# One-core decoder layer: order of the score matmuls, weight halves in slots of their own, convolution taps dealt out anew, the last norm's small matmuls later

## The chip, the cores and the metric

The kernel runs on one core of one Trainium2 chip. The metric is the device time of one execution in microseconds (us), lower is better. Engines are called as in the profile: PE multiplies matrices, DVE, ACT and POOL work on vectors, SP issues most of the DMAs.

## The reference, cut to what matters

One layer over 256 tokens of width 1024, all in float32: a mixer, cross attention and a gated feed-forward part (FFN), each behind an RMS norm.

```
h = rms_norm(x);  x = x + hybrid_mixer(h) ; x = x + cross_attention(rms_norm(x), mem); x = x + swiglu(rms_norm(x))
# hybrid_mixer
(u_conv, q, kc, vc, ks, vs, kw, vw, g_nsa_heads, g_conv, g_attn) = split(h @ w_in)
conv_out = conv_module(u_conv)     # a*sigmoid(g), depthwise causal convolution of 31 taps, layer norm, silu, @ pw_w
nsa_out  = nsa_attention(q, ...)   # 16 heads of 64; compressed, selected and window branch, gated
y = sigmoid(g_conv) * conv_out + sigmoid(g_attn) * nsa_out;   return y @ w_out
# swiglu
a, b = split(h @ w_in);  return (silu(a) * b) @ w_out
```

## The kernel before, in words

**Weights.** A projection is cut into chunks of 256 output columns, named after what they make: k0 to k3, u0 to u7, kc, vc, q0 to q3, ks, kw, vs, vw, ga0 to ga3, gc0 to gc3, pw0 to pw3, wo, xq, v, xo, f0 to f21. Each chunk arrives in two halves (`_0`, `_1`, 512 KB each). `split` (L195) makes two fp32r tiles of a half: ACT copies the high part (`f_0h`, L205), and DVE or POOL subtracts it to leave the low part (`f_0l`, L208). `rows` and `sweep` (L285 to L305, matmuls on L297) then multiply: 8 matmuls of 128x128 by 128x256 for high times high, 8 for high times low input, 8 for low weights times high input; 48 for a chunk. Those of one half are in one row of the views as x8.

**Slots.** Most weight halves rotate through five buffers, `whi` and `wlo`. `set_apart` (L220) gives one half two slots of its own instead, in which the high part begins 64 floats and the low part 112 floats behind the slot's start. Before, these are k3_0, xq1_0, xq2_0, xo0_1, ks_0 and f2_0.

**Order.** `in_line` and `behind` tie matmuls to the one written before them; the rest is placed by a scheduler with priorities, and each engine takes its own instructions in order.

**Scores.** `scores(hp)` (L840) makes the scores of two heads against the keys (kdh, kdl are their high and low parts): `later_half` the second 128 queries of a head (tiles `s`, 512 columns, L852), the loop on L858 the first 128 of both (256 columns each, L860). DVE adds the bias and takes minima (L865, L871), ACT takes the exponential (L886), DVE normalises (L889 to L896), PE transposes the weights (`pt_a`, `pt_b`, L907) and multiplies them with the values (`o`). `scores(0)` stands in front of ga3, later ones stand between pieces of gc and v (v is the value projection of the cross attention).

**Convolution taps.** 8 blocks of 128 channels, 31 taps each, between 30 and 160 us. `taps_v` (L488) is DVE's chain of multiply-adds (L494) with every third product of the later taps from ACT (L486) and an addition on DVE (L508). `taps_g` (L513) is POOL's: products by ACT, additions on L530, for the first ON_G taps of channel blocks 6 and 7. LEAD and the tuple in the call of `convolve` (L570) say how many steps are dealt out behind which u chunk.

**Small fp32 matmuls** interrupt the stream of fp32r ones: the relative bias tables (`rel_ps` L579, `cb_ps` L587), branch gates and compressed scores (`gt_ps` L805, `cs_ps` L793), the norm in front of the FFN (`rn` sums over partitions, L379; `sp` spreads the root, L397) and the 16 transposes of the residual (`fo`, L1236).

Of the kernel before, what the change touches and what calls it, by code (L numbers as in the profile page):

```python
# [118 lines left out]
def tile_hybrid_block(  # L119
# [113 lines left out]
    set_apart("xq1_0", "LL")  # L233
    set_apart("xq2_0", "LL")
    set_apart("xo0_1", "LL")
    set_apart("ks_0", "L11", "L13")
    set_apart("f2_0", "L9", "L0")

    def behind(*marks):
# [118 lines left out]
    def newton(v, name):  # L358

        I32 = mybir.dt.int32  # L360
        g, t = (small(f"{c}_{name}", [P, 2]) for c in ("nr", "nt"))
        nc.vector.tensor_scalar(out=t.bitcast(I32), in0=v.bitcast(I32), scalar1=1, scalar2=None, op0=ALU.arith_shift_right)
        nc.vector.tensor_scalar(out=g.bitcast(I32), in0=t.bitcast(I32), scalar1=-1.0, scalar2=float(0x5F3759DF), op0=ALU.mult,
                                op1=ALU.add)
        for _ in range(4):
            nc.gpsimd.tensor_tensor(out=t, in0=g, in1=g, op=ALU.mult)
            nc.gpsimd.tensor_tensor(out=t, in0=t, in1=v, op=ALU.mult)
            nc.gpsimd.tensor_scalar(out=t, in0=t, scalar1=-0.5, scalar2=1.5, op0=ALU.mult, op1=ALU.add)
            nc.gpsimd.tensor_tensor(out=g, in0=g, in1=t, op=ALU.mult)
        return g  # L370
# [109 lines left out]

    yt = long("yt", 6)

    def product_of(j, t, to, n=2):

        for i in range(n):
            nc.scalar.activation(to[:, i], vt[j + i][:, t:t + S], AF.Identity, scale=col(PP_DW + TAPS * (j + i), t),  # L486
                                 bias=col(PP_DB, j + i) if t == 0 else 0.0)

    def taps_v(j, ts, out, lead=0):

        acc = aux(f"yp{j}", [P, 2, S], "pt", 2)

        def step(i, t, to):
            nc.vector.scalar_tensor_tensor(out=to[:, i], in0=vt[j + i][:, t:t + S], scalar=col(PP_DW + TAPS * (j + i), t),  # L494
                                           in1=acc[:, i], op0=ALU.mult, op1=ALU.add)

        early, late = ts[1:1 + lead], ts[1 + lead:]
        product_of(j, ts[0], acc, 1)
        for t in early:
            step(0, t, acc)  # L500
            yield
        product_of(j + 1, ts[0], acc[:, 1:2], 1)
        for n, t in enumerate(late):
# [37 lines left out]
    def by_turns(a, b, alone):  # L541

        yield from islice(a, alone)
        for _ in a:
# [1 line left out]
            yield next(b, None)  # L546
        yield from b

    on_v = chain(by_turns(taps_v(0, taps, yt[:, 0:2], LEAD), taps_v(2, taps, yt[:, 2:4]), 18 + LEAD),
                 by_turns(taps_v(4, taps, yt[:, 4:6]), taps_v(6, taps[ON_G:], part67), 0))  # L550
    on_g = chain(taps_g(6, taps[:ON_G]), joined(6, part67))

# [12 lines left out]
    for j in range(NB):  # L565
        ps = gemm(f"u{j}", h)
        sg = small(f"sg{j}", [P, S], tag="sg", bufs=3)
        act = nc.scalar.activation(sg, ps[:, 1], AF.Sigmoid)
        vec = nc.vector.tensor_tensor(out=vt[j][:, PAD:], in0=ps[:, 0], in1=sg, op=ALU.mult)
        convolve((LEAD, 8, 10, 10, 10, 10, 10, 10)[j], 0, act, vec)  # L570


    tables = long("tables", 12, (P, RT_END + len(CGROUPS) * P))
# [1 line left out]
    with behind(loads["u6_1"]):  # L575
        nc.sync.dma_start(relt, rel)
        nc.sync.dma_start(cbt, cb)
    rel_ps = aux("rel_ps", [P, 384], "s", 2)
    nc.tensor.matmul(rel_ps, lhsT=relt[:, 0:P], rhs=relt[:, P:512],  # L579
                     start=True, stop=True)  # L580

# [173 lines left out]
            js = slice(j, j + 2)  # L755
            nc.vector.tensor_tensor(out=yt[:, js], in0=yt[:, js], in1=rl.unsqueeze(1).to_broadcast([P, 2, S]), op=ALU.mult)

    def gate(j):

        ps = bank(f"ps_ga{j}")  # L760
        for i in range(2):
            sweep(ps, halved(f"ga{j}", i), h, i)
        return nc.scalar.activation(sga[:, 2 * j:2 * j + 2], ps, AF.Copy if j == 3 else AF.Sigmoid)

    sums = small("sums", [P, HEADS, 2, 2])
# [21 lines left out]
    def compressed_scores(ct):  # L787
# [7 lines left out]
        last[:] = [mm]  # L795
        nc.vector.tensor_tensor(out=nsc, in0=cs_ps, in1=nsc, op=ALU.add)

    four[0] = ""
    ct = compressed_products()
    gate(0)  # L800
    compressed_scores(ct)
    gt_ps = aux("gt_ps", [P, 2, ng], "o", 1)

    for tb in range(2):
        nc.tensor.matmul(gt_ps[:, tb], lhsT=sgn[:, tb * P:tb * P + P], rhs=cpt[:, CP_GS:CP_GS + ng], start=tb == 0, stop=tb == 1)  # L805
    sgt = small("sgt", [P, 2, ng], tag="sg", bufs=3)
    nc.scalar.activation(sgt, gt_ps, AF.Sigmoid)
    nc.vector.reciprocal(igc, sgt[:, :, 0:HEADS])
    vec = nc.vector.reciprocal(igd.rearrange("p h t b -> p t b h"),
                               sgt[:, :, HEADS:3 * HEADS].rearrange("p t (b h) -> p t b h", b=2))  # L810
    vcm = small("vcm", [P, GROUPS, 2, HD], F32R, tag="wg")
    for k in range(2):
        nc.scalar.activation(vcm[:, :, k], f(vcs), AF.Copy, scale=cpt[:, CP_HM + k:CP_HM + k + 1])
    gate(1)
    mark = gate(2)
    stacked = long("stacked", 9, (P, 2, NB, 4, 32), F32R)

# [22 lines left out]
    def scores(hp):  # L840

        g = hp // 2
        nbp = bias_of(hp)
        s0 = aux(f"s0_{hp}", [P, 2, 2, P], "s0", 1)
        p0 = small(f"p0_{hp}", [P, 2, 2, P], tag="p0", bufs=2)
        s1s, p1 = [], []

        def later_half(hd):
            s1 = aux(f"s1_{hd}", [P, 2, S], "s", 2)
            with in_line():  # L850
                for i, t in enumerate((kdh, kdl)):
                    mm = nc.tensor.matmul(s1, lhsT=qh(hd, 1), rhs=t[:, g].rearrange("p b t -> p (b t)"), start=i == 0, stop=i == 1)  # L852
            last[:] = [mm]
            s1s.append(s1)

        later_half(2 * hp)
        for k, hd in enumerate(heads_of(hp)):
            with in_line():  # L858
                for i, t in enumerate((kdh, kdl)):
                    mm = nc.tensor.matmul(s0[:, k], lhsT=qh(hd, 0), rhs=t[:, g, :, 0:P], start=i == 0, stop=i == 1)  # L860
        last[:] = [mm]
        later_half(2 * hp + 1)
        for k, hd in enumerate(heads_of(hp)):
# [12 lines left out]
        return p0, p1  # L876
# [677 lines left out]
```

## Time and profile before

| | |
|---|---|
| median of 3 runs | 531.22 us (530.62 to 531.57) |
| the profiled execution | 528.97 us, of which the span from first to last instruction 527.2 us |
| PE busy in the span | 520.1 us (99%) |
| DVE, ACT, POOL busy | 442.3, 368.4, 147.4 us |
| granted PE clock, mean | 0.997 |

The profiled execution is 2.25 us below the median; differences are worked out in its time and then put on the median. A busy PE means that an instruction is in it, not that it runs at its best rate, so the distance from start to start of the same instructions has to be read beside the busy share.

### The profile page before, as it was taken

The numbers are of one execution on the slowest core, as the hardware profiler recorded it, in microseconds if no ns is written. First come the engines' busy times: TensorE is split into PE (matmuls) and PEld (weight loads), VectorE is DVE, ScalarE is ACT, GpSimd is POOL, SyncE is SP. The second block draws the span as 40 slices with busy tenths as digits, with TensorE's granted clock in tenths as the row PEclk, the third lists the DMA queues.
The fourth block names the chain that finished last, engine by engine and source line by source line (L and its number), as shares of the span: only waits on it lengthen the run. The fifth ranks groups of instructions, "written<-read, shape, count | busy, mean of one in ns | idle before, by whom it ended". The sixth has DMA issues, their size and how long they took to land.

```text
span 527.2 us, 11194 instructions
## 1 busy us (share of the span) xinstructions
PE 520.1 (99%) x4319; PEld 502.4 (95%) x4319; DVE 442.3 (84%) x861; ACT 368.4 (70%) x671; POOL 147.4 (28%) x105
## 2 busy tenths in 40 slices
PE   9999999999999999999999999999999999999995
PEld 8999999999899999999999999999999999988884
DVE  4887899999999999984969685688988786689996
ACT  5678784999967899789648675565665555557743
POOL 0019889999995000330004000310000000000002
PEclk9999999999999999999999999999999999999998
DMA  8947966544545436224667542368665665625402
GB/s 315 410 168 250 322 202 212 165 161 153 166 160 184 160 127 208 88 81 160 222 217 274 192 156 99 109 197 300 229 219 192 197 201 188 201 93 159 162 0 81
DMA packets 29445, 97.20 MB, mean 184 GB/s; under 512 B 3152, under 2 KB 5456, under 8 KB 29136
## 3 DMA queue, kind: packets, MB, share of 16 engines
q1 hardware_dynamic: 28816, 95.44, 53.9%
q10 hardware_dynamic: 576, 1.05, 0.5%
q8 instruction: 34, 0.56, 0.4%
q14 instruction: 19, 0.16, 0.1%
HBM read 95.23 MB, written 1.25 MB: 183 GB/s over the span
## 4 chain that ended last, share of the span: by engine, by line
PE 98%; DVE 1%; ACT 0%; issue 0%; ACTq 0%
PE ps_f L297 23%; PE ps_u L297 8%; PE fo L1313 6%; PE ps_v L297 4%; PE ps_gc L297 4%; PE ps_ga L297 4%; PE ps_q L297 4%; PE ps_xq L297 4%; PE ps_pw L297 4%; PE ps_wo L297 4%; PE fos L1313 4%; PE ps_k L297 3%; PE ps_xo L297 3%; PE ps_xo L1198 2%; PE o L920 1%; PE s L852 1%
## 5 line engine op out<-in xcount | busy, mean ns | idle before, releaser
L494 DVE SCALAR_TENSOR_TENSOR yp<-vt,ppt,yp 128x256 f32<-128x256 f32 x144 | 64.2, 485 | 6.3 <-ACT yp L486 4.6
L1382 POOL TENSOR_TENSOR x<-xs,gf 128x512 f32<-128x512 f32 x2 | 2.6, 1302 | 168.3 <-issue 168.3
L297 PE MATMUL ps_f<-g,f_1h 128*128 128x256 f32 x352 | 44.4, 277 | 0.0
L297 PE MATMUL ps_f<-g,f_0h 128*128 128x256 f32 x352 | 43.9, 277 | 0.0
L297 PEld LDWEIGHTS ps_f<-g,f_1h 128*128 128x128 f32 x352 | 41.9, 188 | 0.0
L297 PEld LDWEIGHTS ps_f<-g,f_0h 128*128 128x128 f32 x352 | 41.8, 188 | 0.0
L205 ACT ACTIVATE f_0h<-f 128x1024 fp32r<-128x1024 f32 x22 | 23.4, 1062 | 18.9 <-issue 15.5
L886 ACT ACTIVATE p<-p,mins 128x128 f32<-128x128 f32 (+1 forms) x64 | 28.3, 449 | 10.2 <-DVE mins L865 10.0
L208 DVE TENSOR_TENSOR f_1l<-f,f_1h 128x1024 fp32r<-128x1024 f32 x22 | 27.4, 1247 | 5.6 <-ACT f_1h L205 5.6
L208 DVE TENSOR_TENSOR f_0l<-f,f_0h 128x1024 fp32r<-128x1024 f32 x22 | 27.3, 1243 | 3.2 <-ACT oxh L346 2.2
L205 ACT ACTIVATE f_1h<-f 128x1024 fp32r<-128x1024 f32 x22 | 23.2, 1060 | 9.4 <-PE ps_f L297 7.9
L486 ACT ACTIVATE vw<-vt,ppt 128x256 f32<-128x256 f32 x60 | 26.6, 499 | 0.6 <-DVE yp L508 0.5
L1272 DVE TENSOR_TENSOR ab<-ps_f,rf 128x512 f32<-128x512 f32 x22 | 15.2, 689 | 11.6 <-PE ps_f L297 11.6
L297 PE MATMUL ps_f<-g,f_1l 128*128 128x256 f32 x176 | 23.6, 277 | 0.0
L297 PE MATMUL ps_f<-g,f_0l 128*128 128x256 f32 x176 | 23.6, 276 | 0.0
L208 POOL TENSOR_TENSOR u_0l<-u,u_0h 128x1024 fp32r<-128x1024 f32 x5 | 12.0, 2404 | 37.5 <-ACT u_0h L205 37.5
L297 PEld LDWEIGHTS ps_f<-g,f_1l 128*128 128x128 f32 x176 | 21.7, 188 | 0.0
L297 PEld LDWEIGHTS ps_f<-g,f_0l 128*128 128x128 f32 x176 | 21.6, 188 | 0.0
L530 POOL TENSOR_TENSOR yt<-yt,vw 128x512 f32<-128x512 f32 x15 | 20.5, 1367 | 0.1
L508 DVE TENSOR_TENSOR yp<-yp,vw 128x512 f32<-128x512 f32 x28 | 19.4, 695 | 0.7
L748 POOL TENSOR_TENSOR ssum<-ssum,sq 128x512 f32<-128x512 f32 x3 | 4.7, 1580 | 44.9 <-ACT sq L747 44.7
L1274 ACT ACTIVATE sl<-ab 128x256 f32<-128x256 f32 x22 | 9.1, 417 | 11.0 <-DVE ab L1272 10.9
(845 smaller groups left out, 1667.4 us busy)
## 6 DMA issues: line engine op xcount, KB each, us to landing
f<-in_wst_dram SPq DMA_DIRECT2D x44, 512.0 KB, 4.4
u<-in_wst_dram SPq DMA_DIRECT2D x14, 512.0 KB, 6.9
for<-in_wfo_dram SPq DMA_DIRECT2D x14, 512.0 KB, 3.8
q<-in_wst_dram SPq DMA_DIRECT2D x8, 512.0 KB, 4.9
ga<-in_wst_dram SPq DMA_DIRECT2D x8, 512.0 KB, 3.3
gc<-in_wst_dram SPq DMA_DIRECT2D x8, 512.0 KB, 3.8
v<-in_wst_dram SPq DMA_DIRECT2D x8, 512.0 KB, 3.1
pw<-in_wst_dram SPq DMA_DIRECT2D x8, 512.0 KB, 4.6
```

The source lines that it names most:

```text
L205: copies = [nc.scalar.activation(hi[:, at:at + n], w[:, at:at + n], AF.Copy) for at in range(0, shape[1], n)]
L208: low = eng.tensor_tensor(out=lo[:, at:at + n], in0=w[:, at:at + n], in1=f(hi[:, at:at + n]), op=ALU.subtract)
L297: mm = nc.tensor.matmul(ps[:, b], lhsT=lhsT, rhs=rhs, start=row + b + kb == 0, stop=kb == NB - 1 and row == 2 and b == 1)
L486: nc.scalar.activation(to[:, i], vt[j + i][:, t:t + S], AF.Identity, scale=col(PP_DW + TAPS * (j + i), t), bias=col(PP_DB, j + i) if t == ...
L494: nc.vector.scalar_tensor_tensor(out=to[:, i], in0=vt[j + i][:, t:t + S], scalar=col(PP_DW + TAPS * (j + i), t), in1=acc[:, i], op0=ALU.mu ...
L508: nc.vector.tensor_tensor(out=to, in0=acc, in1=pr, op=ALU.add)
L530: nc.gpsimd.tensor_tensor(out=y, in0=y, in1=pr, op=ALU.add)
L886: exp.append(nc.scalar.activation(t, t, AF.Exp, scale=-1.0, bias=mins[:, hd, qb, br:br + 1], accum_out=sums[:, hd, qb, br:br + 1]))
L1198: nc.tensor.matmul(qs[:, b], lhsT=parts[m, 1][wi][:, k, cs], rhs=x[xi][:, 4 + k], start=False, stop=k == 3 and row == 2 and b == 1)
L1272: nc.vector.tensor_tensor(out=ab, in0=ps, in1=rf.unsqueeze(1).to_broadcast([P, 2, S]), op=ALU.mult)
L1274: silu = nc.scalar.activation(sl, ab[:, 0], AF.Silu)
L1313: mm = nc.tensor.matmul(o[:, cs], lhsT=t[x], rhs=w[y][:, cs], start=start and n == 0, stop=stop and n == 2)
```

## The change

`scores` issues the four 512-column matmuls of both heads first and ends with the four of 256 columns. q3_0, ga3_0 and pw0_1 get slots of their own, ks_0 goes back to the common ones. `rel_ps` takes another PSUM bank. The branch gates and compressed scores move from between ga0 and ga1 into the middle of ga1. Three taps of channel blocks 6 and 7 go from ACT and POOL to DVE; the first taps of the leading chains are computed by DVE instead of ACT, and the second leading chain leads by 7 instead of 10. One Newton step of four is left out of a reciprocal root on POOL. The norm in front of the FFN is issued inside f0 and f1 rather than in front of them.

```
-ON_G = 16
-LEAD = 10
+ON_G = 13
+LEAD, DEALT = 10, (10, 11, 12, 12, 12, 12, 12, 12)
...
-    set_apart("ks_0", "L11", "L13")
+    set_apart("q3_0", "L11", "L13")
+    set_apart("ga3_0", "L13", "L9")
+    set_apart("pw0_1", "L10", "L14")
...
-        for _ in range(4):
+        for _ in range(3):
...
+        def first_of(j, i, to):
+            nc.vector.tensor_scalar(out=to[:, i], in0=vt[j + i][:, 0:S], scalar1=col(PP_DW + TAPS * (j + i), 0),
+                                    scalar2=col(PP_DB, j + i), op0=ALU.mult, op1=ALU.add)
...
-        product_of(j, ts[0], acc, 1)
+        if lead:
+            first_of(j, 0, acc)
+        else:
+            product_of(j, ts[0], acc)
...
-        product_of(j + 1, ts[0], acc[:, 1:2], 1)
+        if lead:
+            first_of(j, 1, acc)
...
-    on_v = chain(by_turns(taps_v(0, taps, yt[:, 0:2], LEAD), taps_v(2, taps, yt[:, 2:4]), 18 + LEAD),
+    on_v = chain(by_turns(taps_v(0, taps, yt[:, 0:2], LEAD), taps_v(2, taps, yt[:, 2:4], 7), sum(DEALT[:2])),
...
-        convolve((LEAD, 8, 10, 10, 10, 10, 10, 10)[j], 0, act, vec)
+        convolve(DEALT[j], 0, act, vec)
...
-    rel_ps = aux("rel_ps", [P, 384], "s", 2)
+    rel_ps = aux("rel_ps", [P, 384], "o", 1)
...
+    def between_gates():
+        branch_gates()
+        compressed_scores(ct)
...
     gate(0)
-    compressed_scores(ct)
...
+    gate(1, between_gates)
...
         later_half(2 * hp)
+        later_half(2 * hp + 1)
         for k, hd in enumerate(heads_of(hp)):
...
-        later_half(2 * hp + 1)
...
-    rf = small("rf", [P, S], tag="vw", bufs=4)
-    nc.scalar.activation(rf, spread(rnorm(acc2, "3"), "3"), AF.Copy)
...
+    for _ in range(7):
+        next(firsts)
+    with in_line():
+        r3 = rnorm(acc2, "3")
+    for _ in range(5):
+        next(firsts)
+    with in_line():
+        r3 = spread(r3, "3")
```

On PE, at the first scores, between ga2 and ga3 (`s_1` and `s_0` on the 512-column lines are the second halves of the two heads). Before:

```order
L297 MATMUL ps_ga_2154<-hh,ga_1l 128x256 x8
L852 MATMUL s_0_2222<-kdh,qt 128x512
L852 MATMUL s_0_2222<-kdl,qt 128x512
L860 MATMUL s_0_2220<-kdh,qt 128x256
L860 MATMUL s_0_2220<-kdl,qt 128x256
L860 MATMUL s_0_2220<-kdh,qt 128x256
L860 MATMUL s_0_2220<-kdl,qt 128x256
L852 MATMUL s_1_2229<-kdh,qt 128x512
L852 MATMUL s_1_2229<-kdl,qt 128x512
L297 MATMUL ps_ga_2242<-hh,ga_0h 128x256 x8
```

And of the change at the same place:

```order
L299 MATMUL ps_ga_2144<-hh,ga_1l 128x256 x8
L872 MATMUL s_0_2212<-kdh,qt 128x512
L872 MATMUL s_0_2212<-kdl,qt 128x512
L872 MATMUL s_1_2215<-kdh,qt 128x512
L872 MATMUL s_1_2215<-kdl,qt 128x512
L881 MATMUL s_0_2210<-kdh,qt 128x256
L881 MATMUL s_0_2210<-kdl,qt 128x256
L881 MATMUL s_0_2210<-kdh,qt 128x256
L881 MATMUL s_0_2210<-kdl,qt 128x256
L299 MATMUL ps_ga_2232<-hh,ga_0h 128x256 x8
```

The same eight matmuls stand there; the last one in front of the next projection has 256 columns instead of 512.

On PE, from the FFN's first chunk to its third (g is the FFN's input, `fo` the transposes of the residual). Before, the norm's two pieces and all 16 transposes lie ahead of f2:

```order
L297 MATMUL ps_f_4790<-g_4482,f_1h 128x256 x7
L379 MATMUL rn_4764<-ones,acc_4483 128x2 x2
L297 MATMUL ps_f_4790<-g_4482,f_1h 128x256 x6
...
L397 MATMUL sp_4770<-cpt,r_4767 128x128 x2
L297 MATMUL ps_f_4858<-g_4482,f_1h 128x256 x9
L297 MATMUL ps_f_4858<-g_4482,f_1l 128x256 x8
L1236 MATMUL fo_0_4935<-cpt,x_4481 128x128 x4
L1236 MATMUL fo_1_4936<-cpt,x_4481 128x128 x4
L1236 MATMUL fo_0_4937<-cpt,x_4481 128x128 x4
L1236 MATMUL fo_1_4938<-cpt,x_4481 128x128 x4
L297 MATMUL ps_f_4955<-g_4482,f_0h 128x256 x16
```

Of the change, the end of the same place (12 of the transposes have gone ahead into f0):

```order
L399 MATMUL sp_4893<-cpt,r_4844 128x128 x2
L299 MATMUL ps_f_4941<-g_4468,f_0h 128x256 x14
L299 MATMUL ps_f_4941<-g_4468,f_0l 128x256 x8
L299 MATMUL ps_f_4941<-g_4468,f_1h 128x256 x2
L1254 MATMUL fo_0_4923<-cpt,x_4467 128x128 x4
L299 MATMUL ps_f_4941<-g_4468,f_1h 128x256 x14
L299 MATMUL ps_f_4941<-g_4468,f_1l 128x256 x8
```

The last four transposes now lie behind f2_0, the half with slots of its own, and no such half follows in the FFN.

On DVE, the last instructions ahead of the first score reduction (L865, in the change L885; yp and yt belong to the taps). Before:

```order
L208 TENSOR_TENSOR gc_0l<-gc_0_2329,gc_0h 128x1024
L494 SCALAR_TENSOR_TENSOR yp_1277<-vt_368,ppt,yp_1277 128x256 x4
L208 TENSOR_TENSOR gc_1l<-gc_1_2359,gc_1h 128x1024
L508 TENSOR_TENSOR yt<-yp_1277,vw_30_1976 128x512
L208 TENSOR_TENSOR gc_0l<-gc_0_2434,gc_0h 128x1024
L865 ISA p_0_2221,mins<-s_0_2220,nb_2217 128x128
```

Of the change:

```order
L208 TENSOR_TENSOR gc_0l<-gc_0_2319,gc_0h 128x1024
L518 TENSOR_TENSOR yp_1194<-yp_1194,vw_27_1967 128x512
L820 RECIPROCAL igc<-sgt 128x32
L821 RECIPROCAL igd<-sgt 128x4x16
L808 TENSOR_TENSOR nsc<-cs_ps,nsc 128x512
L500 SCALAR_TENSOR_TENSOR yp_1194<-vt_368,ppt,yp_1194 128x256
L208 TENSOR_TENSOR gc_1l<-gc_1_2349,gc_1h 128x1024
L500 SCALAR_TENSOR_TENSOR yp_1194<-vt_368,ppt,yp_1194 128x256 x3
L208 TENSOR_TENSOR gc_0l<-gc_0_2424,gc_0h 128x1024
L518 TENSOR_TENSOR yt<-yp_1194,vw_30_1975 128x512
L208 TENSOR_TENSOR gc_1l<-gc_1_2454,gc_1h 128x1024
L885 ISA p_0_2211,mins<-s_0_2210,nb_2207 128x128
```

One more subtraction for gc, `gc_1_2454`, has moved ahead of the reduction, and with it the reciprocals and `nsc`, which stood further ahead before.

## Rows read from the trace of the kernel before

**Rows 1.** The page: busy time by engine, and the chain that ended last.
```profile
PE 520.1 (99%) x4319; PEld 502.4 (95%) x4319; DVE 442.3 (84%) x861; ACT 368.4 (70%) x671; POOL 147.4 (28%) x105
...
PE 98%; DVE 1%; ACT 0%; issue 0%; ACTq 0%
```

**Rows 2.** Windows: stretch, length, busy PE, PEld, DVE, ACT, POOL (instructions), granted clock, DMA.
```profile
359.00:465.00 106.00, 106.00 (x938) 106.00 (x937) 86.76 (x149) 60.52 (x97) 0.00 (x0) 1.00 0.63 206
```

**Rows 3.** Timeline of PE, q3 and ks: start, us until the end, line, tiles, forms, count.
```profile
104.25 1.19 PE L297 MATMUL ps_q<-hh,q_0h 128*128 128x256 f32 x8
...
109.98 1.12 PE L297 MATMUL ps_ks<-hh,ks_0h 128*128 128x256 f32 x8
...
111.90 1.07 PE L297 MATMUL ps_ks<-hh,ks_0l 128*128 128x256 f32 x8
112.81 1.07 PE L297 MATMUL ps_ks<-hh,ks_1h 128*128 128x256 f32 x8
```

**Rows 4.** The same timeline around scores(0), to the start of scores(1).
```profile
152.13 1.07 PE L297 MATMUL ps_ga<-hh,ga_1l 128*128 128x256 f32 x8
153.04 0.40 PE L852 MATMUL s<-kdh,qt 128*128 128x512 f32 x1
...
154.43 1.11 PE L297 MATMUL ps_ga<-hh,ga_0h 128*128 128x256 f32 x8
...
165.74 0.40 PE L852 MATMUL s<-kdh,qt 128*128 128x512 f32 x1
```

**Rows 5.** The same timeline, kc behind the bias table.
```profile
74.06 1.10 PE L297 MATMUL ps_kc<-hl,kc_0h 128*128 128x256 f32 x8
75.00 1.11 PE L297 MATMUL ps_kc<-hh,kc_0l 128*128 128x256 f32 x8
```

**Rows 6.** The same timeline, v behind scores(4), and the start of pw.
```profile
195.67 1.11 PE L297 MATMUL ps_v<-v_0h,memh 128*128 128x256 f32 x8
196.61 1.10 PE L297 MATMUL ps_v<-v_0h,meml 128*128 128x256 f32 x8
...
257.63 1.98 PE L297 MATMUL ps_pw<-z,pw_0h 128*128 128x256 f32 x16
259.44 1.07 PE L297 MATMUL ps_pw<-z,pw_0l 128*128 128x256 f32 x8
```

**Rows 7.** The same timeline, FFN from the norm to f2.
```profile
348.14 0.50 PE L379 MATMUL rn<-ones,acc 128*128 128x2 f32 x4
...
350.46 1.11 PE L297 MATMUL ps_f<-g,f_0l 128*128 128x256 f32 x8
351.41 0.99 PE L297 MATMUL ps_f<-g,f_1h 128*128 128x256 f32 x7
...
356.35 2.16 PE L297 MATMUL ps_f<-g,f_0h 128*128 128x256 f32 x16
358.34 1.07 PE L297 MATMUL ps_f<-g,f_0l 128*128 128x256 f32 x8
```

**Rows 8.** The same timeline, the transposes of scores(0) and gc1 behind them.
```profile
170.91 0.60 PE L907 MATMUL pt_b<-cpt,p 128*128 128x128 f32 x4
...
173.14 1.07 PE L297 MATMUL ps_gc<-hh,gc_1l 128*128 128x256 f32 x8
174.05 0.40 PE L852 MATMUL s<-kdh,qt 128*128 128x512 f32 x1
```

**Rows 9.** Timeline of DVE, ahead of and behind the first score reductions.
```profile
149.48 4.57 DVE L208 TENSOR_TENSOR gc_0l<-gc,gc_0h 128x1024 fp32r<-128x1024 f32 x1
...
159.69 0.28 DVE L865 CUSTOM_DVE_ANT_0 p<-s,nb 128x128 f32<-128x128 f32 x1
...
168.45 0.28 DVE L896 TENSOR_SCALAR p<-p,sums 128x128 f32<-128x128 f32 x1
```

**Rows 10.** The page's groups of the taps: count, busy us, mean ns, idle before.
```profile
L494 DVE SCALAR_TENSOR_TENSOR yp<-vt,ppt,yp 128x256 f32<-128x256 f32 x144 | 64.2, 485 | 6.3 <-ACT yp L486 4.6
...
L530 POOL TENSOR_TENSOR yt<-yt,vw 128x512 f32<-128x512 f32 x15 | 20.5, 1367 | 0.1
L508 DVE TENSOR_TENSOR yp<-yp,vw 128x512 f32<-128x512 f32 x28 | 19.4, 695 | 0.7
```

More of the change, by code (lines that the diff above doesn't have):

```diff
@@ L481, in tile_hybrid_block, with product_of @@
     yt = long("yt", 6)
-    def product_of(j, t, to, n=2):
-        for i in range(n):
+    def product_of(j, t, to):
+        for i in range(2):
             nc.scalar.activation(to[:, i], vt[j + i][:, t:t + S], AF.Identity, scale=col(PP_DW + TAPS * (j + i), t),
@@ L756, in layer_norm_scale, with gate @@
             nc.vector.tensor_tensor(out=yt[:, js], in0=yt[:, js], in1=rl.unsqueeze(1).to_broadcast([P, 2, S]), op=ALU.mult)
-    def gate(j):
+    def gate(j, between=None):
         ps = bank(f"ps_ga{j}")
@@ L762, in gate @@
             sweep(ps, halved(f"ga{j}", i), h, i)
+            if between and i == 0:
+                between()
         return nc.scalar.activation(sga[:, 2 * j:2 * j + 2], ps, AF.Copy if j == 3 else AF.Sigmoid)
@@ L796, in compressed_scores, with branch_gates @@
         nc.vector.tensor_tensor(out=nsc, in0=cs_ps, in1=nsc, op=ALU.add)
+    def branch_gates():
+        gt_ps = aux("gt_ps", [P, 2, ng], "o", 1)
+        for tb in range(2):
+            with in_line():
+                mm = nc.tensor.matmul(gt_ps[:, tb], lhsT=sgn[:, tb * P:tb * P + P], rhs=cpt[:, CP_GS:CP_GS + ng], start=tb == 0, stop=tb == 1)
+        last[:] = [mm]
+        sgt = small("sgt", [P, 2, ng], tag="sg", bufs=3)
+        nc.scalar.activation(sgt, gt_ps, AF.Sigmoid)
+        nc.vector.reciprocal(igc, sgt[:, :, 0:HEADS])
+        nc.vector.reciprocal(igd.rearrange("p h t b -> p t b h"),
+                                   sgt[:, :, HEADS:3 * HEADS].rearrange("p t (b h) -> p t b h", b=2))
+    def between_gates():
+        branch_gates()
+        compressed_scores(ct)
     four[0] = ""
@@ L800, in tile_hybrid_block @@
     gate(0)
-    compressed_scores(ct)
[L802 to L810, printed above, removed]
+    gate(1, between_gates)
     vcm = small("vcm", [P, GROUPS, 2, HD], F32R, tag="wg")
@@ L813, in tile_hybrid_block @@
         nc.scalar.activation(vcm[:, :, k], f(vcs), AF.Copy, scale=cpt[:, CP_HM + k:CP_HM + k + 1])
-    gate(1)
     mark = gate(2)
@@ L1268, in tile_hybrid_block, with first_products @@
     fgs = fg[:, 0], fg[:, 1]
+    def first_products():
+        for j in range(2):
+            ps = bank(f"ps_f{j}")
+            first_ps.append(ps)
+            for i in range(2):
+                yield from rows(ps, halved(f"f{j}", i), fgs, i)
+    first_ps, firsts = [], first_products()
+    for _ in range(7):
[4 more added lines that the diff above has]
+        next(firsts)
+    with in_line():
+        r3 = spread(r3, "3")
+    rf = small("rf", [P, S], tag="vw", bufs=4)
+    nc.scalar.activation(rf, r3, AF.Copy)
+    for _ in firsts:
+        pass
     for j in range(NF):
-        ps = gemm(f"f{j}", fgs)
+        ps = first_ps[j] if j < 2 else gemm(f"f{j}", fgs)
         ab = small(f"ab{j}", [P, 2, S], tag="pr", bufs=4)
```

## The prediction

> **What bounds the kernel now.** I read the page first: PE is busy 520.1 us of a span of 527.2, and the chain that ended last is PE for 98% [rows 1]. PE hardly waits for anybody, so taking work from DVE, ACT or POOL cannot shorten anything by itself. [...] The change adds and removes no matmul. What is left is the rate at which the same matmul runs, and for that one must leave the busy shares and subtract starts in PE's timeline. The 128x128 by 128x256 matmuls come in blocks of eight, and a block takes one of three times, all at granted clock 1.00:
>
> - **fast**, 0.91: from 111.90 to 112.81 in ks [rows 3], from 152.13 to 153.04 ahead of scores(0) [rows 4];
> - **slow**, 0.94: from 74.06 to 75.00 in kc [rows 5], from 195.67 to 196.61 in v [rows 6];
> - **slowest**, 0.96: ks_0h, the half with a slot of its own, from 109.98 to 111.90 for two blocks [rows 3].
>
> I use 0.907, 0.942 and 0.959 (long fast stretches: 16 matmuls from 257.63 to 259.44 take 1.81 [rows 6]; 12 slow blocks from 154.43 to 165.74 take 11.31 [rows 4]; 1.92 for 16 [rows 3]). So a fast matmul costs 0.0044 us less than a slow one and 0.0065 less than a slowest one.
>
> The rate belongs to stretches, not to tiles. It changes at interruptions: from fast to slow across scores(0) [rows 4], slow in q3 up to ks_0h and fast at once behind it [rows 3], slow behind the norm's small matmul, then slowest in f2_0h (from 356.35 to 358.34, 1.99 for 16, with some 0.07 of start-up) and fast behind it [rows 7]. Twice the same thing, then: 16 matmuls of a high half with its own slot pay 0.05 a block over fast, and everything behind it is fast. Transposes can do it too: behind those of scores(0), gc_1l runs from 173.14 to 174.05, fast [rows 8]. What decides inside PE, the trace does not show; I argue from these pairs.
>
> **The change part by part.** Sums go against the profiled 528.97 us, 2.25 us under the median; the difference is then put on the median.
>
> *q3_0 apart, ks_0 not.* q3 and ks_0h take 7.65 us now (104.25 to 111.90, 64 matmuls) [rows 3]. After: q3_0h slowest, two blocks; q3_0l, q3_1 and ks_0h, six blocks, fast. Eight slow blocks would be 7.54, so 0.11 is start-up and the dearer ks_0h: before is 0.08 start-up + 6 x 0.942 + 1.92 = 7.65, after 0.08 + 1.92 + 6 x 0.907 = 7.44. **-0.21.**
>
> *ga3_0 apart.* From 154.43 to 165.74 lie 12 slow blocks [rows 4]. After: two slowest and ten fast, 1.92 + 9.07 = 10.99. **-0.32.** If the stretch behind a slot of one's own is not fast here, it is +0.03.
>
> *rel_ps in another bank.* The four cb_ps products move ahead of kc, so the 28 kc matmuls that are slow now [rows 5] follow a piece of another kind; they were fast behind it before. 28 x 0.0044: **-0.12**, at worst 0 (slow all the same).
>
> *pw0_1 apart.* pw is fast already [rows 6], so here the slot only costs: 16 x 0.0065, **+0.10**. It pays only if the new score order leaves pw slow, and then it gives no more than what is lost first.
>
> *Score order.* The same eight matmuls, 1.39 us now (153.04 to 154.43) [rows 4]. What can change is the rate behind them. Behind scores(0) to scores(3) weights of ga and gc follow, as kc's and f's do, from the common slots; I keep them slow, except as above. Behind scores(4) to scores(7) the weights are the moving operand (v): 3, 4, 3 and 2 slow blocks directly behind them, the first from 195.67 [rows 6], 96 matmuls. In all, 192 matmuls of v are slow between 195.67 and 241. No run shows matmuls of 256 columns as the last ones. Bounds: 0, and 192 x 0.0044 = -0.85. I take the half directly behind the scores, **-0.42**, because the interruptions in between are transposes, which [rows 8] shows can end a slow stretch but not that they keep a fast one.
>
> *Norm and transposes spread in the FFN.* Slow now are the blocks from rn at 348.14 to f2 (350.46 to 351.41 is 0.95 [rows 7]), 48 matmuls. After, some 29 behind the early transposes and 40 from rn to f2 may be slow, 21 more: 0 to +0.09; five interruptions instead of three, at most the 0.07 of [rows 7] each: 0 to +0.14. I take **+0.10**.
>
> *Branch gates inside ga1.* The same six matmuls at another place. ga1 and ga2 are fast behind them now and may stay so, 0, or turn slow for 72 matmuls up to scores(0), +0.32. I take 0.
>
> *Taps.* Counted in the order: DVE gets 10 multiply-adds and 4 first products more, 2 additions less: 14 x 0.485 - 2 x 0.695 = +5.4 us (a first product taken as dear as a multiply-add); POOL loses 3 additions, 3 x 1.367 = -4.1 us [rows 10]; ACT loses 14 products. What hides DVE's 5.4 is the 6.3 us that it sits idle ahead of its multiply-adds, 4.6 of them for ACT's first products [rows 10], which the leading chains no longer need. I take **0**. Without this cover DVE comes late to the score reductions; the price is below. The Newton step less takes four small instructions from POOL, for which PE does not wait: 0.
>
> Sum: -0.21 - 0.32 - 0.12 + 0.10 - 0.42 + 0.10 = **-0.87 us**, 528.1 for the profiled execution and **530.35** for the median. About 0.2%, 1.06 us, is what a measurement of this kernel can tell from no change; the forecast lies within it.
>
> [...] ks_0h and ks_0l are multiplied alike, and take 0.96 and 0.91 a block [rows 3]. [...]
>
> **The rivals.**
>
> 1. *v stays slow.* Ending on 256 columns changes nothing. -0.45: 530.8. For it: scores(0) and scores(4) leave different operands and yet the same slow rate [rows 4, 6].
> 2. *The score order does more.* All 192 matmuls of v are fast: -1.30, 529.9. If gc's 88 slow ones behind scores(1) to scores(3) are fast too, another 88 x 0.0044 = 0.39: -1.69, 529.5. Against it: what follows there are common slots, as in the slow kc [rows 5].
> 3. *The FFN turns slow: slower than before.* The last four transposes now lie inside f2_1h, behind the one half that makes the FFN fast [rows 7], and nothing behind them would mend it. From 359 to 465 there are 938 matmuls [rows 2]; less the first some 14, 924 x 0.0044 = +4.1, with the rest of the sum +3.2: 534.4. It decides as soon as more than some 440 of these matmuls are slow. For it: the norm's matmul turned a fast stretch slow at 348.14 [rows 7]. Against it: transposes of the same form left gc_1l fast [rows 8], though that stretch came in slow.
> 4. *Rates do not follow the slots.* Only the interruptions count: 0 to +0.14, 531.3.
> 5. *DVE late at the scores: slower.* The first reduction starts at 159.69, behind taps and gc's subtractions, the last normalising ends at 168.73, and PE takes the transposes at 170.91 [rows 8, 9]: 2.2 us of slack. In the change one more subtraction stands ahead (about 1.6) and 5.4 us of taps. If nothing of the idle time is won back, DVE is 7.0 late, PE stands 4.8, with the rest of the sum +3.9: 535.1. It decides from 4.1 us late on (2.2 slack, 0.87 gain, 1.06 bound). Against it: besides the idle 6.3, the subtraction gc_0l took 4.57 at 149.48, a time when POOL was busy too [rows 9], and POOL now has 4.1 us less to do.
>
> **How the numbers follow.** Chances: forecast 0.45, rival 1 0.17, rival 2 0.15, rival 3 0.11, rival 4 0.07, rival 5 0.05. The predicted time is the forecast's, 530.35. The terms' bounds within it (v 0 to -0.85, kc 0, ga3 +0.03, gates +0.32) and the spread of the median itself, 530.62 to 531.57, make some +-0.8, 529.5 to 531.2. For 8 in 10 the range takes in rival 2 with its bound below and rivals 1 and 4 above with theirs: 528.9 to 532.1; rival 3 and rival 5 stay outside. Faster by over 0.2% (under 530.16): nearly all of rival 2 and some 0.4 of the forecast, with a little of rival 1: 0.35. Slower by over 0.2%: rivals 3 and 5 and a little of 4: 0.17. Within: 0.48.
>
> **What would show it.** Starts in PE's timeline, per block of eight: q3_0h 0.96, then 0.91 to the end of ks; ga3_0h 0.96 and 0.91 from ga3_0l to scores(1), about 11.0 us; kc 0.91 throughout; pw0_1h 0.96; v directly behind scores(4) 0.91 (0.94 is rival 1); f3 to f21 0.91 (0.94 is rival 3, which makes the prediction wrong by itself); PE idle ahead of pt_b and a first reduction later than about 162 is rival 5. Also wrong it would be if PE waited for q3_0l or ga3_0l because their slots come free late: each must have been made ahead of its first matmul, at about 106 and 156 us, and a wait there would stand in PE's list of waits, which now has nothing in these stretches.

## The result, and the profile after

The change makes the kernel **slower**: median 534.03 us (531.41 to 535.69, 6 runs) against 530.92 (529.26 to 531.57, 6 runs); ratio 1.0057, 95% interval 1.0032 to 1.0081. The forecast was 530.35 and its range ended at 532.1.

The profiled execution took 533.79 us, 4.82 more than that of before. The page has PE busy for 521.9 us of a span of 532.0, so PE is idle for 10.1 us of it, 3.0 more than before [rows 1]. The list of PE's waits (engine and line, what it waited for, total us, times, longest):

```profile
PE s L872 <- DVE nsc L808: 2.6, 1, 2.6
...
PE s L872 <- ACT pct L1006: 0.4, 1, 0.4
```

Beside the warm-up there are two waits, and both are the scores': a large one in scores(0), a small one in scores(7). `nsc` is DVE's addition that takes the compressed scores out of their PSUM bank `cs_ps`. PE's timeline in scores(0) (start, us, line, tiles, count; in brackets the idle time ahead and what ended it):

```profile
152.52 1.07 PE L299 MATMUL ps_ga<-hh,ga_1l 128*128 128x256 f32 x8
...
153.66 0.40 PE L872 MATMUL s<-kdl,qt 128*128 128x512 f32 x1
156.61 0.50 PE L872 MATMUL s<-kdh,qt 128*128 128x512 f32 x1 [2.56 <-DVE nsc L808]
...
157.66 1.54 PE L299 MATMUL ps_ga<-hh,ga_0h 128*128 128x256 f32 x8
159.00 1.91 PE L299 MATMUL ps_ga<-hl,ga_0h 128*128 128x256 f32 x8
160.70 1.48 PE L299 MATMUL ps_ga<-hh,ga_0l 128*128 128x256 f32 x8
162.02 1.07 PE L299 MATMUL ps_ga<-hh,ga_1h 128*128 128x256 f32 x8
```

Two losses stand in these rows, where [rows 4] had eight score matmuls in a row and then 0.94 a block. First the wait: from the first head's scores to ga3 it takes 4.23 us (153.43 to 157.66) instead of 1.39, 2.84 more. Then three blocks of ga3 take 1.34, 1.70 and 1.32. The windows over these blocks (columns as in [rows 2]; the granted clock is the third number from the end) say why:

```profile
157.66:159.00 1.34, 1.34 (x11) 1.34 (x10) 1.30 (x3) 0.92 (x1) 0.00 (x0) 0.67 0.99 400
159.00:160.70 1.70, 1.70 (x9) 1.70 (x9) 1.67 (x3) 1.50 (x3) 0.00 (x0) 0.50 0.98 357
160.70:162.00 1.30, 1.30 (x9) 1.30 (x9) 1.30 (x3) 1.28 (x2) 0.38 (x1) 0.68 0.76 265
162.00:165.00 3.00, 3.00 (x29) 3.00 (x28) 2.83 (x17) 2.33 (x10) 2.51 (x2) 1.00 0.85 285
```

The granted clock is 0.50 in the second row and 0.67 and 0.68 in the rows beside it, after PE had been idle for 2.56 us. From 162 on it is 1.00 again, as it was from 156.60 to 157.66. At 0.96, 0.96 and 0.91 the three blocks would have taken 2.83 instead of 4.36: **1.53 us** for the clock. Together 4.37 of the 4.82.

Why did the second head's scores wait for `nsc`? DVE's timeline:

```profile
147.75 6.99 DVE L208 TENSOR_TENSOR gc_0l<-gc,gc_0h 128x1024 fp32r<-128x1024 f32 x1
...
155.94 0.62 DVE L808 TENSOR_TENSOR nsc<-cs_ps,nsc 128x512 f32<-128x512 f32 x1
...
159.66 1.22 DVE L208 TENSOR_TENSOR gc_0l<-gc,gc_0h 128x1024 fp32r<-128x1024 f32 x1
...
162.53 0.28 DVE L885 CUSTOM_DVE_ANT_0 p<-s,nb 128x128 f32<-128x128 f32 x1
```

The compressed scores `cs_ps` lie in one of the two PSUM banks `s`, and so do the second halves of the scores. `nsc` reads that bank and frees it. It now stands behind a gc_0l that takes 6.99 us, where the next one takes 1.22, and frees the bank at 156.56. PE's next matmul starts at 156.61. POOL was busy with TENSOR_TENSOR operations for nearly all of that time. Its timeline in the change, then in before:

```profile
146.36 4.81 POOL L208 TENSOR_TENSOR ga_1l<-ga,ga_1h 128x1024 fp32r<-128x1024 f32 x2
...
152.31 1.35 POOL L540 TENSOR_TENSOR yt<-yt,vw 128x512 f32<-128x512 f32 x1
153.74 2.12 POOL L544 TENSOR_TENSOR yt<-yt,part 128x512 f32<-128x512 f32 x1
```

```profile
151.62 1.34 POOL L530 TENSOR_TENSOR yt<-yt,vw 128x512 f32<-128x512 f32 x1
153.04 2.16 POOL L724 TENSOR_TENSOR ysum<-yt 128x512 f32<-128x512 f32 x1
```

These rows show what the length of gc_0l goes with. POOL's first pause behind its start is at 153.66 in the change and at 152.96 in before, each time for 0.08 us, and gc_0l ends 1.08 and 1.09 us behind that, at 154.74 and at 154.05. In all 14 profiles, those of the two kernels and of the twelve runs, this first gc_0l ends 1.07 to 1.09 us behind the start of that pause, wherever it began. So in these profiles it lasted for as long as POOL went on without a pause, and some 1.1 us more; the next gc_0l of the change, at 159.66, when POOL was idle, took 1.22 in all.

The rates changed too. The timeline of PE at four places, in order of time: kc behind the bias tables, the end of q3, gc behind scores(1), v behind scores(5):

```profile
75.19 1.10 PE L299 MATMUL ps_kc<-hl,kc_0h 128*128 128x256 f32 x8
76.13 1.11 PE L299 MATMUL ps_kc<-hh,kc_0l 128*128 128x256 f32 x8
...
104.91 1.20 PE L299 MATMUL ps_q<-hh,q_0h 128*128 128x256 f32 x8
...
112.34 1.07 PE L299 MATMUL ps_ks<-hh,ks_0l 128*128 128x256 f32 x8
...
171.58 1.07 PE L299 MATMUL ps_gc<-hh,gc_0h 128*128 128x256 f32 x8
172.49 1.07 PE L299 MATMUL ps_gc<-hl,gc_0h 128*128 128x256 f32 x8
...
208.92 1.07 PE L299 MATMUL ps_v<-v_0h,memh 128*128 128x256 f32 x8
209.83 1.07 PE L299 MATMUL ps_v<-v_0h,meml 128*128 128x256 f32 x8
```

q3 and ks_0h take 7.43 (104.91 to 112.34) against 7.65 [rows 3]; gc is fast (0.91) behind scores(1) to scores(3), v behind scores(5) to scores(7), and kc, vc and q0, of which all but the first 28 matmuls were fast, are slow (0.94). Summed between the same matmuls of the two profiles: first loads +0.19, bias tables to q3 +0.47, q3 -0.23, ga1 and ga2 -0.06, scores(0) to scores(1) +4.05, to scores(4) -0.39, to pw +0.46, pw +0.11, f0 to f2 +0.20: 4.80.

### The profile page after: what moved, and what is told of

Its sections match the earlier page's. It is cut to its first block, busy times and chain, and to the rows that moved or that the text cites. A ratio compares the mean times of both kernels' runs of the same rounds, so it can differ in the third digit from the quotient of the medians.

```text
span 532.0 us, 11171 instructions
## 1 busy us (share of the span) xinstructions
PE 521.9 (98%) x4319; PEld 502.9 (95%) x4319; DVE 445.8 (84%) x873; ACT 362.6 (68%) x657; POOL 141.0 (27%) x98
## 4 chain that ended last, share of the span: by engine, by line
PE 84%; DVE 11%; ACT 4%; issue 1%; DVEq 0%; ACTq 0%
PE ps_f L299 23%; PE ps_u L299 8%; PE fo L1353 6%; PE ps_xq L299 4%; PE ps_pw L299 4%; PE ps_gc L299 4%; PE ps_wo L299 4%; PE fos L1353 4%; DVE yp L500 3%; PE ps_k L299 3%; PE ps_v L299 3%; PE ps_xo L299 3%; PE ps_q L299 2%; PE ps_xo L1218 2%; PE ps_ga L299 1%; DVE gc_0l L208 1%
## 5 line engine op out<-in xcount | busy, mean ns | idle before, releaser
L488 ACT ACTIVATE vw<-vt,ppt 128x256 f32<-128x256 f32 x56 | 24.7, 500 | 0.7 <-POOL yt L540 0.5
L518 DVE TENSOR_TENSOR yp<-yp,vw 128x512 f32<-128x512 f32 x27 | 18.1, 691 | 0.4
L540 POOL TENSOR_TENSOR yt<-yt,vw 128x512 f32<-128x512 f32 x12 | 15.8, 1314 | 2.1 <-ACT vw L538 1.9
```

The costliest lines, as they stand in the source:

```text
L540: nc.gpsimd.tensor_tensor(out=y, in0=y, in1=pr, op=ALU.add)
```

## The experiments

Each of the twelve is the changed kernel with the edit shown, or that of before where it says so. Theory A: the late `nsc`, behind gc_0l, costs the time. Ratios are to the kernel before on the same chip, with 95% intervals.

**nsc first.** `first_low` makes one subtraction come behind `nsc`; PE's order is untouched.

```
+                with behind(*first_low.get(name, ())):
...
+        first_low["gc0_0"] = nc.vector.tensor_tensor(out=nsc, in0=cs_ps, in1=nsc, op=ALU.add),
```

> The changed kernel with one instruction moved on DVE: the subtraction gc_0l comes behind the addition nsc instead of ahead of it; PE's order is the same. Theory A (nsc frees the PSUM bank that the second head's scores need; it stood behind a gc_0l of 6.99 us, PE idled 2.56 us, and the clock then fell): nsc ends by about 150, no wait at the scores, granted clock 1.00 from 154 to 170, three blocks of ga3 at 0.96, 0.96 and 0.91 instead of 1.34, 1.70 and 1.32; the profiled execution 533.79 - 2.9 - 1.5 = about 529.4, the median near 529.5, faster than before by 0.2 to 0.3%. Theory B (DVE is late as a whole because of the taps, and whatever stands last pays): the wait moves to the score transposes, 1 to 3 us, and the median stays above 531.5. Theory C (the slow blocks come from the weight slots of ga3_0, not from the idle time): the wait goes, the slow blocks stay, about 531.

Measured: 530.01 (529.34 to 530.77, 12 runs), ratio 0.9982 (0.9968 to 0.9996). Timelines of DVE, then of PE:

```profile
147.85 0.63 DVE L809 TENSOR_TENSOR nsc<-cs_ps,nsc 128x512 f32<-128x512 f32 x1
148.40 4.97 DVE L209 TENSOR_TENSOR gc_0l<-gc,gc_0h 128x1024 fp32r<-128x1024 f32 x1
```

```profile
153.82 0.40 PE L873 MATMUL s<-kdl,qt 128*128 128x512 f32 x1
...
154.53 1.11 PE L300 MATMUL ps_ga<-hh,ga_0h 128*128 128x256 f32 x8
155.48 1.12 PE L300 MATMUL ps_ga<-hl,ga_0h 128*128 128x256 f32 x8
156.44 1.07 PE L300 MATMUL ps_ga<-hh,ga_0l 128*128 128x256 f32 x8
```

One instruction moved on DVE takes back the whole loss: no wait, granted clock 1.00 from 154 to 170, and ga3_0h, ga3_0l at 0.95, 0.96, 0.91. Theory A holds; theory B (no wait took its place at the transposes) and theory C (same slots, no blocks of 1.3 to 1.7) fall.

**PE kept busy while it waits.** The first head's score matmuls of scores(0) eight times over.

```
-                for i, t in enumerate((kdh, kdl)):
+                for i, t in enumerate((kdh, kdl) * (8 if hd == 0 else 1)):
+                    i = i % 2
```

> The changed kernel with the first head's score matmuls of scores(0) made eight times over (14 matmuls of 512 columns more, the same result), so that PE works while it would wait for the bank. 14 x 0.234 = 3.28 us of work against 2.9 us of waiting. Theory A (idle time lets the clock fall): no idle time, clock 1.00, ga3_0h at 0.96 a block, the execution 0.4 later up to ga3 and 1.6 earlier behind it: about 1.2 us faster than the change, median near 532.8 for a change at 534.0. Theory C (the slow blocks come from the slots): clock and blocks as in the change, 0.4 us slower than it, 534.4.

Measured: 533.21 (532.48 to 533.99, 9 runs), ratio 1.0035 (1.0023 to 1.0048), 0.0022 or 1.2 us below the change's, as theory A said; the two intervals overlap, but the profiles agree: 15.57 us from scores(0) to scores(1) against 16.75. The blocks of ga3 are normal although they begin 4.59 us behind the first score matmul, 0.36 later than in the change (timeline of PE):

```profile
159.23 1.12 PE L299 MATMUL ps_ga<-hh,ga_0h 128*128 128x256 f32 x8
...
161.15 1.07 PE L299 MATMUL ps_ga<-hh,ga_0l 128*128 128x256 f32 x8
```

With work in place of the idle time the clock stayed at 1.00, and the useless work was cheaper than waiting. One pair of profiles does not show that the idle time is the cause, since the clock does not fall behind every wait (below). The executions together point to it: a mean granted clock under 0.996 stands in four of the six of the change (0.991 to 0.995) and in three of the six with the taps as before (0.991 to 0.994; PE waits 2.69 us there, see below), and in none of the 200 others of before and of these experiments. In the change those four took 533.79 to 535.69 us, the other two 531.41 and 532.64.

**Gates back between ga0 and ga1.**

```
     gate(0)
-    gate(1, between_gates)
+    compressed_scores(ct)
+    branch_gates()
```

> The changed kernel with branch gates and compressed scores back between ga0 and ga1, all else as changed. Theory A: cs_ps is there 3.5 us earlier and nsc stands ahead of gc_0l, so no wait and no fall of the clock: as with nsc first, near 529.5. Theory B (taps make DVE late): the wait moves to the score transposes and the median stays above 531.5.

Measured: 530.29 (529.42 to 531.15, 12 runs), ratio 0.9986 (0.9974 to 0.9999). No wait at scores(0): as theory A said.

**Taps as before**, gates still in the middle of ga1.

```
-ON_G = 13
+ON_G = 16
...
```

> The changed kernel with the taps as before (ON_G 16, LEAD 10, first products on ACT), gates in the middle of ga1 as changed. In its order nsc stands ahead of gc_0l. Theory A: no wait at the scores; near 529.5 to 530. Theory B (taps): the same, so this run parts A and B only together with the two others. If it still waits 2 to 3 us at the scores, the moved gates are to blame by themselves.

Measured: 536.02 (534.27 to 537.34, 6 runs), ratio 1.0088 (1.0068 to 1.0109): the slowest of all, against what I expected. Timeline of PE:

```profile
159.90 1.07 PE L299 MATMUL ps_ga<-hh,ga_1l 128*128 128x256 f32 x8
163.66 1.20 PE L299 MATMUL ps_gc<-hh,gc_0h 128*128 128x256 f32 x8 [2.69 <-ACT sga L767]
164.70 1.07 PE L299 MATMUL ps_gc<-hl,gc_0h 128*128 128x256 f32 x8
```

The scores of scores(0) do not wait, `nsc` stands ahead of gc_0l as its order said; but gc_0l takes 6.82 us again (from 150.26), ACT waits 5.1 us behind it for a product that DVE must use up first, and so frees the PSUM bank of gc0 late (`sga`). It is the same instruction, with another victim. Here PE idled longer than in the change, and yet the blocks behind it are fast in this execution. The new taps have a part in the wait for `nsc`, since with the old ones `nsc` stands ahead of gc_0l; but taking them back does not make the change faster.

**The gates alone**, on the kernel before (the diff's lines for `branch_gates`, `between_gates` and `gate`).

> The kernel before with one part of the change alone: branch gates and compressed scores in the middle of ga1. In its order nsc stays ahead of gc_0l. If the wait needs the taps as well (they put gc_0l ahead of nsc), no wait at the second head's scores here, and the time is that of before within 0.2%, 531. If moving the gates is enough, nsc comes late and PE waits 2 to 3 us at the scores: 533 to 535. With the old taps in the changed kernel PE waited 2.69 us at gc0; if that is due to the gates, it shows here too, 533.5 to 536.

Measured: 530.30 (529.33 to 532.71, 12 runs), ratio 1.0003 (0.9988 to 1.0018): no change, and no wait for `nsc`. Moving the gates is not enough.

**Taps, gates and slots together**, on the kernel before.

```
-    set_apart("ks_0", "L11", "L13")
+    set_apart("q3_0", "L11", "L13")
+    set_apart("ga3_0", "L13", "L9")
...
```

> The kernel before with three parts of the change: taps, gates inside ga1, and the slots of q3_0 and ga3_0; score order, bias table's bank, pw0_1, the FFN's norm and the Newton steps as before. Its order puts gc_0l ahead of nsc. Theory A: PE waits for nsc ahead of the second head's scores, 0.47 us less than in the change since they come later here: 2.1 us, the clock falls behind it in some executions; 533 to 534. If the score order is needed, no wait, and 530.5.

Measured: 532.69 (531.54 to 534.12, 12 runs), ratio 1.0017 (1.0001 to 1.0034). Timeline of PE:

```profile
157.24 0.50 PE L871 MATMUL s<-kdh,qt 128*128 128x512 f32 x1 [1.63 <-DVE nsc L807]
...
157.81 1.12 PE L298 MATMUL ps_ga<-hh,ga_0h 128*128 128x256 f32 x8
...
159.72 1.07 PE L298 MATMUL ps_ga<-hh,ga_0l 128*128 128x256 f32 x8
```

The wait is there without the new score order, 0.9 shorter: the order of the scores gave 0.47 of that, and one of DVE's additions (some 0.6) stands ahead of gc_0l here instead of between it and `nsc`. The clock did not fall behind it: 0.96 and 0.91. The time is a little below what I expected, for that reason.

**ga3_0 in the common slots.**

```
-    set_apart("ga3_0", "L13", "L9")
```

> The changed kernel with ga3_0 in the common slots; in its order nsc stands ahead of gc_0l by itself. Theory A: no wait at the second head's scores although gates, taps and score order are as changed; 530.0 to 530.6. If it waits as the changed kernel does, theory A falls. For the rates: ga3 and gc0 behind scores(0) slow (12 blocks, 11.31) if the score order does nothing for common slots, 10.88 if it does.

Measured: 530.44 (528.62 to 531.29, 12 runs), ratio 0.9971 (0.9953 to 0.9989). Timeline of PE:

```profile
155.12 1.07 PE L298 MATMUL ps_ga<-hh,ga_0h 128*128 128x256 f32 x8
156.03 1.07 PE L298 MATMUL ps_ga<-hl,ga_0h 128*128 128x256 f32 x8
...
166.00 0.40 PE L871 MATMUL s<-kdh,qt 128*128 128x512 f32 x1
```

Without these slots `nsc` comes ahead of gc_0l and nothing waits at scores(0). And the 12 blocks take 10.88, fast from the first: with the new score order ga3 is fast without its slots. There they only cost their 0.1, and, through the scheduler's order, the wait.

**The old score order, with nsc first.**

```
         later_half(2 * hp)
-        later_half(2 * hp + 1)
...
+        later_half(2 * hp + 1)
```

> The changed kernel with nsc first and the old score order. If the score order makes what follows fast, gc behind scores(1) to scores(3) goes back from 0.907 to 0.942 a block (88 matmuls, +0.39) and v behind scores(5) to scores(7) too (+0.3), while the wait of 0.39 us ahead of the second head of scores(7) goes (-0.5): +0.2 us against the kernel with nsc first, 530.2. If the order does nothing for the rate: -0.5, 529.5.

Measured: 530.02 (529.47 to 531.51, 12 runs), ratio 0.9989 (0.9975 to 1.0002): no difference from the new order that the medians can show. In the profile both of the expected things are there and nearly cancel: gc and v are slow as in before, and the wait in scores(7) is gone. ga3 stays at 12.37 us from scores(0) to scores(1): with the old order its slots make it fast.

**The kernel before once more**, unchanged, one execution.

> The kernel before, unchanged, for a second profile. Its first profile took 528.97 us, its median is 531.0, and the changed kernel with nsc first, whose matmul rates in the trace sum to 0.4 us more than in the first profile of before, has a median 0.9 below it. Theory D: typical executions of before hold waits of PE that the first profile did not hold, behind the same DVE subtraction gc_0l (4.57 us there, 6.99 in the change); then an execution near 531 shows 1 to 3 us of PE idle between 154 and 175 and the same rates. Theory E: the spread lies in the first 30 us, in the first loads; then PE's first u chunk starts 1 to 2 us later and nothing else differs.

Measured: 532.72, 3.75 above the first profile and 2.3 above the median of before on that chip (530.42), so it is one of its slow executions as the first was one of its fast ones. The list of PE's waits has one at the transposes, then PE's timeline in pw:

```profile
PE pt_b L907 <- DVE mins L865: 0.4, 1, 0.4
```

```profile
243.20 3.71 PE L297 MATMUL ps_pw<-z,pw_0h 128*128 128x256 f32 x30
246.75 1.11 PE L297 MATMUL ps_pw<-z,pw_0l 128*128 128x256 f32 x8
...
259.24 1.10 PE L297 MATMUL ps_pw<-z,pw_1l 128*128 128x256 f32 x8
```

First loads +1.44, a wait of 0.4 at the transposes +0.5; and pw and wo run slow throughout, where they were fast in [rows 6]: 22.63 and 22.61 against 21.81 and 21.76, +1.67. Theories D and E both have a part, and the largest part is one that neither named. The same program, the same slots: the rate of a stretch differs from one execution to the next. The profile of the gates alone (532.71, the slowest of its 12) has the same 22.63 and 22.61.

**pw0_1 apart, alone**, on the kernel before.

```
+    set_apart("pw0_1", "L10", "L14")
```

> The kernel before with pw0_1 in slots of its own, nothing else. In the first profile of before pw and wo were fast, in the second (532.72 us) slow throughout, 0.82 and 0.85 us more, until the next half with slots of its own. If a typical execution of before is like the second, the slots end that: pw and wo slow only for pw0_0, at most 0.25 above fast; the median 0.5 to 1.4 us below before, and fewer executions above 531.5. If pw is fast as a rule, the slots cost 0.1 and the time is that of before.

Measured: 531.04 (529.90 to 532.29, 12 runs) beside 531.71 for before on that chip, ratio 0.9982 (0.9968 to 0.9996); 2 of its 12 executions lie above 531.5, and 21 of the 31 of before. In its profile pw came in slow and left fast (timeline of PE):

```profile
247.10 1.11 PE L298 MATMUL ps_pw<-z,pw_0l 128*128 128x256 f32 x8
248.04 0.40 PE L298 MATMUL ps_pw<-z,pw_1h 128*128 128x256 f32 x2
...
250.07 1.07 PE L298 MATMUL ps_pw<-z,pw_1l 128*128 128x256 f32 x8
250.98 0.73 PE L298 MATMUL ps_pw<-z,pw_0h 128*128 128x256 f32 x5
```

pw takes 22.03 and wo 21.76. The slots are an insurance: 0.1 where the stretch is fast anyway, and some 1.4 back where it is not.

**Trimmed.** nsc first; `rel_ps` in its old bank, pw0_1 in the common slots, the FFN's norm and scores(7) as before.

```
-    rel_ps = aux("rel_ps", [P, 384], "o", 1)
+    rel_ps = aux("rel_ps", [P, 384], "s", 2)
...
-    set_apart("pw0_1", "L10", "L14")
...
+        if hp == 7:
+            later_half(2 * hp + 1)
```

> The changed kernel with nsc first, and without the parts whose rows cost: rel_ps in its old bank (q0 to q2 and vc fast again, -0.4 against the kernel with nsc first), pw0_1 in the common slots (-0.25), the norm in front of the FFN as before (-0.2), scores(7) in the old order (-0.5 for the wait). If these rows add up, -1.3: the median near 528.7, faster than before by 0.4%. If rates flip elsewhere in turn, between 529.3 and 530.

Measured: 529.61 (528.62 to 530.37, 12 runs), ratio 0.9981 (0.9966 to 0.9995). By its ratio it is no better than nsc first (0.9982); its median is 0.4 lower, but that of before was 0.6 lower on this chip. The 1.3 did not come. The old bank did not bring q0 to q2 back: from vc to kc_ps it takes 24.82 here, 24.42 with the new bank, 24.00 in before. `cb_ps` also stands seven matmuls of kc later here than in before. The other three gave what their rows said.

**Trimmed, with vc_0 and pw0_1 apart**, and `rel_ps` in the new bank: the version that the rows point to.

```
+    set_apart("vc_0", "L11", "L10")
```

> The best version that the rows point to: the changed kernel with nsc first, the order of before for scores(7) and for the FFN's norm, and one more half with slots of its own, vc_0, to end the slow stretch that kc, vc and q0 have had behind the bias tables in every profile of the changed kernel. vc_0h 0.96 a block, then 0.91 to q3: 24.10 from vc to kc_ps against 24.42 (nsc first) and 24.82 (trimmed). Against the trimmed kernel (529.61) -0.7 there and +0.1 for pw0_1: 529.0. If rates flip back behind z_ps, 529.6.

Measured: **529.40** (528.75 to 530.81, 8 runs) beside 531.71 for before, ratio 0.9954 (0.9938 to 0.9969): faster than before, and so than the change. Timeline of PE at vc:

```profile
80.68 1.12 PE L301 MATMUL ps_vc<-hh,vc_0h 128*128 128x256 f32 x8
81.64 1.12 PE L301 MATMUL ps_vc<-hl,vc_0h 128*128 128x256 f32 x8
82.60 1.07 PE L301 MATMUL ps_vc<-hh,vc_0l 128*128 128x256 f32 x8
83.51 1.07 PE L301 MATMUL ps_vc<-hh,vc_1h 128*128 128x256 f32 x8
```

Slowest for two blocks, then fast up to q3 (24.10 from vc to kc_ps), and no wait of PE but the warm-up.

## Why the prediction was wrong

**The step that failed** is the one on the gates: "The same six matmuls at another place. ga1 and ga2 are fast behind them now and may stay so, 0, or turn slow for 72 matmuls up to scores(0), +0.32. I take 0." It counted matmuls and left out what reads their result. `cs_ps` holds a bank that scores(0) needs, `nsc` on DVE frees it, and the order of the change showed `nsc` and the reciprocals behind gc_0l; I quoted these rows and drew nothing from them. An estimate was at hand in the trace of before: gc_0l begins at 149.48 and takes 4.57 [rows 9], the addition, the two reciprocals and `nsc` take some 1.8 more, so `nsc` would end at about 155.8, and the second head's scores would come at 153.5 [rows 4]. That is a wait of some 2.3 us, before any clock. The measured terms in its place: 2.84 us for the wait and 1.53 for the clock. The step also failed by pricing each part alone: the late `nsc` needs the moved gates, ga3's slots and the new taps together, for with any one of them taken back `nsc` stands ahead of gc_0l.

**Rival 5** looked at the right engine and the wrong place: DVE late at the first score reduction, with PE paying at the transposes. DVE was 2.84 later there (162.53 against 159.69), and there was no wait at pt_b, since PE was late too. Its remark on gc_0l was nearly the cause: I took POOL's lighter load as help, but gc_0l ended 1.08 and 1.09 us behind the start of POOL's next pause; it began 1.73 us earlier than in before and that pause came 0.70 us later, so it took 6.99 instead of 4.57.

**Rival 3** did not come: behind the last transposes the FFN is fast to its end (0.91 a block in the change, from 366.79 on). Rival 4 falls: halves with slots of their own were slowest at once and fast behind wherever the clock was 1.00, vc_0 and pw0_1 among them. The part of rival 2 that I argued against came: gc behind scores(1) to scores(3) is fast.

**The terms of the rates**, from the profile with nsc first, where no wait disturbs them:
- q3: -0.21 forecast, -0.23 measured.
- ga3: -0.32 forecast and -0.32 measured (12.70 to 12.38 from scores(0) to scores(1)). The blocks come as argued, with the old score order too (12.37); but with the new order ga3 is fast without the slots (12.28, -0.42), so there they cost 0.10.
- Score order: -0.42 forecast for v. v is fast behind scores(5) to scores(7) and slow behind scores(4); from scores(4) to scores(7) it got -0.15. gc behind scores(1) to scores(3), put at 0, got -0.39. It also costs 0.66 at scores(7) (2.08 for its matmuls instead of 1.42; 0.4 stands in the list of waits), where the second head's matmuls now come before ACT has emptied the bank.
- Bias tables: -0.12 forecast, +0.47 measured. kc stays slow behind cb_ps and hands its rate on to vc and q0. What decides the rate behind an fp32 piece stays open, and the new bank alone is not it: the trimmed kernel and the one with taps, gates and slots together have the old bank and are slower still, +0.87 from rel_ps to kc_ps.
- FFN's norm: +0.10 forecast, +0.21 measured.
- pw0_1: +0.10 forecast, +0.11 in the profile of the change and +0.25 here, where pw came in slow; but over all executions a gain, as its own run shows.
- Taps: 0 forecast. PE has no wait at the transposes in the nine profiles with the new taps, and one of 0.4 in four of the five with the old ones, so there they help a little. Before, only the first chain led, by 10; the second one's 7 is new.

These sum to +0.4 in the profiles, and yet nsc first is 0.18% faster in the medians, near the 0.87 us that I forecast. That is luck in good part and no proof of the sum. The first profile of before was one of its fastest executions (528.97 of 528.8 to 534.7), and a part of the difference may be that executions of before can have a wait at the transposes and a pw and wo that are slow throughout, which no profile with the new taps has; the share of such executions was not measured.

## What to carry to other kernels

When work is moved, follow its result to the instruction that frees its buffer, look at what stands ahead of that one on its engine in the new order, and price it; here that was a DVE subtraction beside a busy POOL, which took 4.57 to 6.99 us instead of 1.22 and ended 1.07 to 1.09 us behind the start of POOL's next pause. A wait of PE can cost more than its own length, here 1.53 us of clock on top of 2.84; if it can't be avoided, useless matmuls in the gap can be cheaper, here by 1.2 us. And a rate read in one profile is one execution's: look at a second before a tenth of a per cent is argued from it.

## What the runs showed of the hardware

The same fp32r matmul at granted clock 1.00 runs at 0.91, 0.94 or 0.96 us for eight, in stretches whose rate can differ between executions of one program (pw and wo, 1.67 us). A weight half offset in slots of its own ran at 0.96 and left 0.91 behind it each time (ks_0 from 109.98 and xq1_0 from 287.55 in before, q3_0 in the change, vc_0 in the last run).

A DVE subtraction of 128x1024 took 1.22 us while POOL was idle (159.66 in the change) and 4.57 to 6.99 while POOL was busy without a pause; it ended 1.07 to 1.09 us behind the start of POOL's first pause, and the POOL instruction behind the pause took 2.12 us in the change where one of that size took 1.35 just before. DVE's multiply-adds beside the same POOL work were not drawn out like that: four of them took 2.06 us from 146.70 in before and from 145.78 in the change. Why the subtraction is and they are not, no run shows.

Idle time of 2.56 us was followed by a granted clock of 0.50 to 0.68 from 157.66 to 162.00 in the profile of the change; behind 1.63 us with taps, gates and slots together and 2.69 us with the taps as before the blocks took 0.96 and 0.91, and 1.04 for the first of gc0, in the executions profiled. The mean clock of the change's six executions, 0.991 to 0.998, suggests that it fell in most but not in all, and so does that of the six with the taps as before, 0.991 to 0.999; only one of each has a trace. Why a wait of that length is followed by a lower clock in some executions only stays open.
